# A Trainium2 encoder block: sums of weights and lower parts of keys change engine, and two products change places

## The chip, the cores and the metric

One core of a Trainium2 chip runs the kernel. The metric is the device time of one execution in microseconds (us). Three executions of the kernel before took 1936.4, 1937.48 and 1934.06 us; the median is 1936.4. TensorE (PE in the profile) multiplies matrices, VectorE (DVE) and ScalarE (ACT) and GpSimd (POOL) work elementwise, SyncE (SP) issues most of the DMAs.

## The reference

One layer of an encoder: RMS norm, one wide projection, two branches (banded attention, and retention with rotated queries and keys), gates, output projections and a last norm. It is all float32, with 2048 rows and a width of 1024.

```
h = rms_norm(x, norm_gain)
proj = einsum('bsd,df->bsf', h, w_in)          # w_in: 1024 x 7168
q_a, k_a, v_a, g_a, q_r, k_r, v_r, g_r, m_a, m_r = split_columns(proj)
o_a = chunk_band_attention(q_a, k_a, v_a, rel_bias)
branch_a = einsum('bsf,fd->bsd', o_a * silu(g_a), w_out_attn)
qr, kr = rotary(q_r, positions), rotary(k_r, positions)
o_r = retention_chunkwise(qr, kr, v_r, gn_gain)
branch_r = einsum('bsf,fd->bsd', o_r * silu(g_r), w_out_ret)
mixed = sigmoid(m_a) * branch_a + sigmoid(m_r) * branch_r
out = rms_norm(x + einsum('bsd,de->bse', mixed, w_out), final_gain)
```

The change lies in the projection (the einsum with w_in) and in what is done to the rotated keys after it.

## The kernel before

**Exact products from two parts.** Every float32 operand of a matmul is held as an upper part, rounded to the format that PE multiplies fast (names with `wh_`, `h_`; made by a cast on ACT), and a lower part, the rest (`wl_`, `l_`; a subtraction on DVE, for some products on POOL). A product uses three of the four combinations: upper times upper, upper times lower, lower times upper.

**Seven products for eight.** The dense multiplications are done by Strassen's method in Winograd's form (class `Strassen`). For the projection a chunk is 256 columns of w_in, a half of the rows of x is one job, and the quarters of the weight chunk are 4 x 128 rows by 128 columns (128x512 on the chip). Four *sums of weights* are built from the quarters: t1 = b12 - b11, t2 = b22 - t1, t3 = b12 - b22, t4 = b21 - t2 (`SUMS_OF`, made in `sum`, L338). Each product n multiplies one quarter or sum with one of seven operands made from x (`R[m]`, in the traces `r`, an even number for an upper part and the next odd one for its lower part): n = 0 uses b11, 1 uses t2, 2 uses t3, 3 uses b21, 4 uses t1, 5 uses t4, 6 uses b22. A product has twelve matmuls of 128x512: four steps, of which each reads one quarter of R's upper and lower part. It writes a PSUM bank that is named after its place: n = 0 and then 3 write x, 1 writes y, 2 writes v, 4 and then 6 write z, 5 writes w. `gather` takes the banks out: ACT copies x into u2 after n = 0, and DVE adds y, v, z and w into u2, u3 and c22. A bank that is used a second time must have been read first: n = 3 waits for the copy of x, n = 6 for c22 (or, in a job with a different order, for whatever read z).

**Jobs.** w_in's columns are done in four jobs: `p0` (what the two branches need, for the first half of the rows: ten chunks), `g0` (gates of that half, 14 chunks, dense work between attention and retention), then `p1` and `g1` for the second half. In p0 and p1 the chunks 3 and 5 (and in p0 the first two) are of other kinds (`Rows`, `Front`), whose sums of weights are on DVE already. The trace leaves numbers out, so that p0's and p1's chunks are both `p`: a sum is `t_p`, the raw weights `raw_p`.

**Order.** The dense products of all jobs stand in one list, `seq`; `dense` runs through it. Ahead of each product it emits the loads and the sums and parts of a product some places later (`prime`, `prepare`, three ahead). Each load is due at a fixed number of places ahead of the chunk's first product (`begins[...]`); p1's first chunk has its own places, at - 9 and at - 6 (L640). What is deferred by `later` comes out after a number of steps, a step being a quarter of a product. All engines run their instructions in program order, and each queue waits at its head.

**Where p1 begins.** At the end of g0 chunk 13 (`g_13`) the operands R, too, are filled anew, from the second half of the rows: a DMA brings them (`r <- cs`), ACT casts the upper parts, and DVE subtracts in place for the lower parts (`r_81 <- r_81,r_80` and so on, four pieces for each of seven). p1's first two chunks are done together, product by product.

**Rotated keys.** In p0 and p1 the keys of the retention branch are rotated (`ep_rotated`) in place, on DVE. Then `parted` makes their parts: ACT copies the upper part (`h_k`), and `low` subtracts the lower part (`l_k`) on the engine that it is given, DVE for queries and POOL for keys, and issues the DMAs that store both. `turn` transposes the keys on PE into a bank of its own, which ACT and DVE empty into `kdt_k`. The rotated parts of keys feed the state of the retention in `krs` and `kds`.

Of the kernel before, what the change touches and what calls it, by code (L numbers as in the profile page):

```python
# [16 lines left out]
ALU = mybir.AluOpType  # L17
# [56 lines left out]
def hybrid_kernel(  # L74
# [30 lines left out]
    def r32(ap):  # L105
        return ap.bitcast(F32)
# [7 lines left out]
    def E(name, dt=F32, shape=(P, 512)):  # L114
        return epool[0].tile(list(shape), dt, tag="e", name=name)

    def TR(name):
        return xpool[0].tile([P, 512], F32, tag="tr", name=name)

    def D(name, shape, dt=F32):  # L120
        return dram.tile(list(shape), dt, name=name)
# [31 lines left out]
    pe, act, dve, pool = Ordered(nc.tensor), Sometimes(nc.scalar), Sometimes(nc.vector), Sometimes(nc.gpsimd)  # L153
# [23 lines left out]
    krscr = [[D(f"krs_{c}_{b}", [2, 2, 4, 32, 2, T], F32R) for b in range(NB)] for c in range(2)]  # L177
    qrscr = [[D(f"qrs_{c}_{b}", [2, 4, 32, 2, 2, T], F32R) for b in range(NB)] for c in range(2)]
# [66 lines left out]
    def later(n, fn):  # L245

        order[0] += 1
        deferred.append((steps[0] + n, order[0], fn, free[0]))
        deferred.sort(key=lambda e: e[:2])
# [8 lines left out]
    def put(lag, dst, src):  # L258

        later(lag, lambda: dma(dst, src))  # L260
# [75 lines left out]
    class Strassen(Chunk):  # L336
# [5 lines left out]
        def sum(self, dst, one, two, ring=None):  # L342
            b = self.b
            if dst in b:
                return
            name = f"{dst}_{self.job.name}_{self.c}"
            t = wp.tile([P, 4, P], F32, tag="t", bufs=SUMS, name=name) if ring is None else \
                ring(name).rearrange("p (k c) -> p k c", k=4)
            b[dst] = self.shaped(t)
            pool.tensor_tensor(b[dst], b[one], b[two], ALU.subtract)  # L350

        def before(self):

# [257 lines left out]
    seq = []  # L611

    def prime(n):

        while ready[0] < min(n, len(seq)):
            _, ch, k = seq[ready[0]]
            ch.prepare(k)
            ready[0] += 1
            if ahead[0] and strict[0] and ready[0] + 1 < len(seq):
                _, ch, k = seq[ready[0] + 1]  # L620
                if isinstance(ch, Strassen):
                    ch.sums(k)

    def dense(jobs):
        chunks = [ch for job in jobs for ch in job.chunks]
        following = dict(zip(chunks, chunks[1:]))
        starts = [k for k, (job, ch, n) in enumerate(seq) if isinstance(ch, Plain) and ch.at(n)[2] == 0]
        count, begins = {}, {}
        for at, (job, ch, n) in enumerate(seq):
            if isinstance(ch, Strassen):  # L630
                begins.setdefault(ch, at)
        sooner = {at - lead: (ch, [j]) for ch, at in begins.items()
                  for j, lead in enumerate(ROW_LEADS if isinstance(ch, Rows) else RAW_LEADS)}
        one, two_, three = jobs[2].chunks[:3]
        for ch in (one, two_, three):
            for lead in RAW_LEADS:
                sooner.pop(begins[ch] - lead)
        two_.raw, three.raw = [], []
        at = begins[one]
        sooner[at - 9], sooner[at - 6] = (one, [0]), (one, [1])  # L640

        first_out = jobs[-1].chunks[0]
        at = begins[first_out]
        for lead in RAW_LEADS:
            sooner.pop(at - lead)
        sooner[at - 8], sooner[at - 5] = (first_out, [0]), (first_out, [1])
        operands = {begins[ch] - 2: ch for ch in begins if ch.job.before}
        for at, (job, ch, n) in enumerate(seq):
            free[0] = job.name[0] == "g"
            count[ch] = count.get(ch, 0) + 1  # L650
            if at in sooner:
                ch2, js = sooner[at]
                if ch2.raw is None or js[0]:
                    len(ch2.raw or ()) == js[0] and ch2.load(js)
            if count[ch] == job.when + 1 and ch in following and following[ch].raw is None and not isinstance(ch, Rows):
                following[ch].load()
            prime(at + ahead[0] + 1)
            while starts and starts[0] <= at + job.lead:
                _, ch2, n2 = seq[starts.pop(0)]
                ch2.before(n2)  # L660
            if at in operands:
                operands[at].before()
            for _ in ch.product(n):
                yield True
                free[0] = job.name[0] == "g"
            for fn in hooks.get((job.name, ch.c, n), ()):
                fn()
            yield True
# [326 lines left out]
    def halves(t):  # L995
        return r32(t).rearrange("p (u n) -> p u n", u=2)

    def two(name, shape=(P, 512)):
        return [E(f"{n}_{name}", F32R, shape) for n in "hl"]
# [100 lines left out]

        return epilogue

    def parted(xs, nm, at, eng, dst):

        ws = {}

        def high(n):
            ws[n] = two(f"{nm}_{n}")
            act.copy(ws[n][0], xs[n])

        def low(n):
            eng.tensor_tensor(ws[n][1], xs[n], r32(ws[n][0]), ALU.subtract)
            for i in range(2):
                put(PUT, dst(i, n), halves(ws[n][i]))

        for n in range(2):
            later(at + n, lambda n=n: high(n))
            later(at + 4 + 2 * n, lambda n=n: low(n))

    def queries(cc, b, xs, nm, late):  # L1120
        parted(xs, nm, late + 9, dve, lambda i, h: r32(qrscr[cc][b][:, :, :, h, i]).rearrange("u i c t -> (i c) u t"))

    def keys(cc, b, xs, nm, late):
        parted(xs, nm, late + 9, pool, lambda i, h: r32(krscr[cc][b][:, i, :, :, h]).rearrange("u i c t -> (i c) u t"))

        def turn(u):
            pk = TR(f"trkr_{nm}_{u}")
            v = pk.rearrange("p (t i c h) -> p t h i c", t=2, i=4, h=2)
            for t in range(2):
                for h in range(2):  # L1130
                    pe.transpose(v[:, t, h], xs[h][:, (2 * u + t) * P:(2 * u + t + 1) * P], ident)
            pk = pk.rearrange("p (t i d) -> p i t d", t=2, i=4)
            kt = []

            def high(n):
                kt.append(E(f"kdt_{nm}_{u}_{n}", F32R, (P, 2, 2, P)))
                act.copy(kt[n][:, :, :, 0:HD], pk[:, 2 * n:2 * n + 2])

            def low(n):
                dve.tensor_tensor(  # L1140
                    kt[n][:, :, :, HD:P], pk[:, 2 * n:2 * n + 2], r32(kt[n][:, :, :, 0:HD]), ALU.subtract
                )
                put(PUT, r32(kdscr[2 * cc + n][b][:, u]), r32(kt[n]).rearrange("p i t c -> p i (t c)"))

            for n in range(2):
                later(2 + n, lambda n=n: high(n))
                later(5 + n, lambda n=n: low(n))

        for u in range(2):
            later(late + 18 + 4 * u, lambda u=u: turn(u))  # L1150
# [719 lines left out]
    end, at = {}, 0  # L1870
# [4 lines left out]
    def hook(name, c, n, fn):  # L1875
        hooks.setdefault((name, c, n), []).append(fn)
# [14 lines left out]
    for n, m in ((4, 4), (5, 5), (6, 2), (7, 6)):  # L1891
        hook("br1", 3, n, lambda n=n, m=m: place_wo(m, *((1, 1) if n < 6 else (n - 4, 2))))

    stream = [dense(jobs)]
    seq.extend((job, ch, n) for job in jobs for ch, n in job.seq)
    for j in (jobs[0], jobs[2]):
        for i in range(2):
            hook(j.name, i, 1 if j is jobs[2] else (0, 1, 1), lambda j=j, i=i: j.chunks[2].load([i]))
# [50 lines left out]
    for key in ("b11", "b12", "b21", "b22"):  # L1949
        ch.b[key] = E(f"{key}_p1", shape=(P, 4, P))  # L1950
        j, h = int(key[1]) - 1, int(key[2]) - 1
# [83 lines left out]
```

## Time and profile before

| | before |
|---|---|
| median of three executions | 1936.4 us |
| the profiled execution | 1934.51 us |
| its span | 1932.7 us |
| DVE, ACT, POOL busy | 70%, 48%, 46% |
| instructions in the span | 31908 |

Times of instructions are given from the span's start. In the page and in the views below, a tile's name without numbers stands for a group; `DVE l_k` is an instruction that writes l_k. In a row of the timeline the brackets give how long the engine was idle ahead of it and what released it: `[1.52 <-DVE c_g L143]`. All instructions carry L143, the line of the helper that records them, so one goes by tiles. `x2` joins two instructions, and the time is that of both. Matmuls overlap; what counts for PE is the distance from one start to the next.

### The profile page before, as it was taken

Reading aid. Unit: us, or ns where it says so; the run is one execution under the profiler, and the core shown is the slowest. Engines: PE = TensorE matmul, PEld = TensorE weight load, DVE = VectorE, ACT = ScalarE, POOL = GpSimd, SP = SyncE. Lnnn points to the kernel's source line nnn. Section 1 sums busy time; section 2 is a strip of 40 time slices with the busy share of each in tenths; the row PEclk is TensorE's granted clock in tenths of the full one; section 3 lists DMA queues with packets and bytes.
Section 4 is the critical chain, followed back from the end, with each engine's and each line's share of the span. In section 5 each row is a group of like instructions: output and inputs, shape, how many; then the busy total and the mean of one; then the engine's idle time right before and its main releaser. Section 6 shows DMA issues by size and latency. Waiting matters only on the chain. (4 is left out here: it accounts for less than half of the span.)

```text
span 1932.7 us, 31908 instructions
## 1 busy us (share of the span) xinstructions
PE 1877.7 (97%) x10437; PEld 1614.5 (84%) x10437; DVE 1353.5 (70%) x2530; ACT 931.1 (48%) x1931; POOL 885.1 (46%) x733
## 2 busy tenths in 40 slices
PE   7999999999999999999999999999999999998998
PEld 6899889888888887899889888888888878886886
DVE  6979788677756558879797777775555654557665
ACT  7555554666655545343333556664555221223554
POOL 0313515546546664223515444544564115547775
PEclk9999999999999999999999999999999999999999
DMA  6586876565659988675666555555998999976673
GB/s 196 165 269 204 264 262 223 182 192 171 173 158 282 272 243 286 197 252 186 206 236 216 161 162 175 161 157 161 290 269 270 323 345 328 325 262 222 208 236 132
DMA packets 325557, 435.93 MB, mean 226 GB/s; under 512 B 29880, under 2 KB 191184, under 8 KB 325392
## 3 DMA queue, kind: packets, MB, share of 16 engines
q1 hardware_dynamic: 260096, 368.35, 59.6%
q10 hardware_dynamic: 65296, 65.55, 11.1%
q8 instruction: 83, 1.36, 0.3%
q14 instruction: 82, 0.67, 0.1%
HBM read 288.14 MB, written 145.64 MB: 224 GB/s over the span
## 5 line engine op out<-in xcount | busy, mean ns | idle before, releaser
L143 POOL TENSOR_SCALAR pr<-pr,rsum 128x640 f32<-128x640 f32 (+4 forms) x128 | 96.1, 751 | 213.7 <-DVE ptl L143 104.8
L143 PE MATMUL ps_g_z<-r,wh_g 128*128 128x512 f32 x448 | 143.7, 402 | 2.7 <-DVE c_g L143 2.7
L143 PE MATMUL ps_g_x<-r,wh_g 128*128 128x512 f32 x448 | 143.2, 401 | 1.2 <-ACT u_g L143 1.1
L143 DVE CUSTOM_DVE_ANT_0 pr<-wide,bt 128x640 f32<-128x640 f32 (+4 forms) x128 | 94.3, 736 | 62.4 <-PE wide L143 55.6
L143 ACT ACTIVATE pr<-pr,mn 128x640 f32<-128x640 f32 (+4 forms) x128 | 98.0, 766 | 81.4 <-DVE mn L143 81.4
L143 DVE TENSOR_TENSOR ptl<-tp,pth 128x384 fp32r<-128x384 f32 x168 | 96.1, 573 | 41.3 <-ACT pth L143 37.4
L143 ACT CAST pth<-tp 128x384 fp32r<-128x384 f32 x168 | 84.5, 515 | 68.5 <-PE tp L143 65.6
L143 POOL TENSOR_TENSOR l_vr<-vrt,h_vr 128x512 fp32r<-128x512 f32 x32 | 47.2, 1476 | 117.0 <-ACT h_vr L143 69.3
L143 POOL TENSOR_TENSOR sl<-sm,sh 128x384 fp32r<-128x384 f32 x64 | 70.4, 1099 | 58.3 <-ACT sh L143 46.3
L143 PEld LDWEIGHTS tp<-ident,pr 128*128 128x128 f32 x560 | 71.2, 140 | 27.3 <-POOL pr L143 2.8
L143 PE MATMUL po<-pth,va 128*128 128x256 f32 x336 | 92.5, 296 | 1.2 <-DMA va<-vas 0.7
L143 POOL TENSOR_TENSOR wl_g<-t_g,wh_g 128x512 fp32r<-128x512 f32 x56 | 75.0, 1339 | 39.9 <-ACT wh_g L143 33.2
L143 PE MATMUL tp<-ident,pr 128*128 128x128 f32 x560 | 89.1, 272 | 3.0 <-POOL pr L143 1.9
L143 ACT CAST wh_p<-raw_p 128x512 fp32r<-128x512 f32 x111 | 68.0, 619 | 49.9 <-PE ps_p_y L143 15.5
L143 DVE TENSOR_TENSOR wl_p<-raw_p,wh_p 128x512 fp32r<-128x512 f32 x111 | 86.2, 783 | 7.4 <-ACT wh_p L143 6.9
L143 DVE TENSOR_TENSOR sm<-sr,dm 128x384 f32<-128x384 f32 x64 | 35.6, 556 | 78.5 <-DMA dm<-in_dmask_dram 28.2
L143 PE MATMUL wide<-ka,qa 128*128 128x384 f32 (+1 forms) x448 | 88.3, 313 | 2.2 <-DVE mn L143 2.1
L143 PEld LDWEIGHTS wide<-ka,qa 128*128 128x128 f32 x448 | 74.6, 188 | 18.6 <-DVE mn L143 8.7
L143 PE MATMUL po<-ptl,va 128*128 128x256 f32 x336 | 88.3, 284 | 1.4 <-DVE ptl L143 0.2
L143 PE MATMUL ps_g_x<-r,wl_g 128*128 128x512 f32 x224 | 88.2, 394 | 0.0
L143 PE MATMUL ps_g_z<-r,wl_g 128*128 128x512 f32 x224 | 88.1, 393 | 0.0
L143 PEld LDWEIGHTS ps_g_x<-r,wh_g 128*128 128x128 f32 x448 | 75.8, 189 | 10.7 <-ACT u_g L143 2.5
(930 smaller groups left out, 6217.3 us busy)
## 6 DMA issues: line engine op xcount, KB each, us to landing
raw_g<-in_w_in_dram ACTq DMA_DIRECT2D x56, 512.0 KB, 5.1
raw_p<-in_w_in_dram ACTq DMA_DIRECT2D x50, 512.0 KB, 5.7
qa<-qas SPq DMA_DIRECT2D x128, 128.0 KB, 3.1
qr<-qrs SPq DMA_DIRECT2D x128, 128.0 KB, 4.6
vr<-vrs SPq DMA_DIRECT2D x64, 256.0 KB, 5.4
ka<-kas SPq DMA_DIRECT2D x56, 256.0 KB, 3.2
va<-vas SPq DMA_DIRECT2D x40, 256.0 KB, 3.3
kds<-kdt_k SPq DMA_DIRECT2D x32, 256.0 KB, 3.3
```

The lines of the kernel that those rows point to most:

```text
L143: return tc.keep_in_program_order(op(*a, **k))
```

## The change

It has three parts.

1. In `Strassen.sum`, the sums of weights of the jobs whose name begins with p (`lean`) are subtracted on DVE instead of POOL. There are 56 of them: t1 to t4 of six chunks of p0 (2, 4, 6, 7, 8, 9) and eight of p1 (0, 1, 2, 4, 6, 7, 8, 9). The gates' sums stay on POOL.
2. In `parted`, the lower part is subtracted on DVE always. This moves the 16 `l_k`.
3. In `seq`, where g0 ends and p1 begins, six entries change places: the last product of the gates, g_13's n = 6, goes behind the first of p_0, and the second of p_1 (n = 3) behind p_0's n = 1. p1's first product is thus one place earlier, so `begins[one]` is smaller by one, and the two leads of its raw loads go from 9 and 6 to 8 and 5, which leaves the loads where they were.

```diff
@@ sum @@
-            pool.tensor_tensor(b[dst], b[one], b[two], ALU.subtract)
+            (dve if self.lean() else pool).tensor_tensor(b[dst], b[one], b[two], ALU.subtract)
+
+        def lean(self):
+            return self.job.name[0] == "p"
@@ dense @@
         at = begins[one]
-        sooner[at - 9], sooner[at - 6] = (one, [0]), (one, [1])
+        sooner[at - 8], sooner[at - 5] = (one, [0]), (one, [1])
@@ parted, queries, keys @@
-    def parted(xs, nm, at, eng, dst):
+    def parted(xs, nm, at, dst):
...
-            eng.tensor_tensor(ws[n][1], xs[n], r32(ws[n][0]), ALU.subtract)
+            dve.tensor_tensor(ws[n][1], xs[n], r32(ws[n][0]), ALU.subtract)
...
-        parted(xs, nm, late + 9, dve, lambda i, h: ...)     # queries
+        parted(xs, nm, late + 9, lambda i, h: ...)
...
-        parted(xs, nm, late + 9, pool, lambda i, h: ...)    # keys
+        parted(xs, nm, late + 9, lambda i, h: ...)
@@ where the jobs are put in a row @@
     seq.extend((job, ch, n) for job in jobs for ch, n in job.seq)
+    at = end["g0"] // 4
+    seq[at - 1:at + 5] = [seq[at + k] for k in (0, -1, 1, 2, 4, 3)]
```

On DVE, at the end of p0 where `trkr_k` is emptied (before the transposes of 247 us), the moved instructions stand as follows. `t1_p0_9` to `t4_p0_9` are the sums for chunk 9 and `l_k_1_0_n` the lower parts of the keys.

```order
 L143 TENSOR_TENSOR wl_p0_9_0_3162<-raw_p0_9_0_2970,wh_p0_9_0_3161 128x512
 L143 SCALAR_TENSOR_TENSOR l_qa_0_2_3201<-ps_p0_8_x_3032,h_qa_0_2_3200 128x512
+L143 TENSOR_TENSOR l_k_1_0_0_3181<-xk_1_0_0_2967,h_k_1_0_0_3180 128x512
 L143 TENSOR_TENSOR kdt_k_1_1_1_0_3193<-trkr_k_1_1_1_3167,kdt_k_1_1_1_0_3193 128x4x64
 L143 TENSOR_TENSOR kdt_k_1_1_1_1_3209<-trkr_k_1_1_1_3167,kdt_k_1_1_1_1_3209 128x4x64
 L143 TENSOR_TENSOR u3_p0_8_3147<-ps_p0_8_w_3216,u3_p0_8_3147 128x512
+L143 TENSOR_TENSOR l_k_1_0_1_3190<-u2_p0_7_2846,h_k_1_0_1_3189 128x512
 L143 TENSOR_TENSOR wl_p0_9_4_3214<-t1_p0_9_3082,wh_p0_9_4_3213 128x512
+L143 TENSOR_TENSOR t4_p0_9_3254<-raw_p0_9_1_3000,t2_p0_9_3084 128x512
```

The added rows stand in DVE's one queue now, ahead of evacuations (kdt_k, u3) that used not to stand behind them.

At chunk 4 of p0, at about 115 us, DVE's queue is:

```order
 L143 TENSOR_TENSOR kdt_k_0_0_1_0_1586<-trkr_k_0_0_1_1553,kdt_k_0_0_1_0_1586 128x4x64
 L143 TENSOR_TENSOR wl_p0_3_5_1_1574<-raw_p0_3_10_1092,wh_p0_3_5_1_1573 128x512
+L143 TENSOR_TENSOR t1_p0_4_1619<-raw_p0_4_0_1432 128x512
+L143 TENSOR_TENSOR t2_p0_4_1621<-raw_p0_4_1_1477,t1_p0_4_1619 128x512
 L143 TENSOR_TENSOR kdt_k_0_0_1_1_1595<-trkr_k_0_0_1_1553,kdt_k_0_0_1_1_1595 128x4x64
 L143 TENSOR_TENSOR c22_p0_3_0_1636<-ps_p0_3_z_0_1576,u3_p0_3_0_1539 128x512
```

The sum t2 needs the second half of the raw weights (`raw_p0_4_1`), and a kdt_k and c22 stand behind it.

On PE, where g0 ends and p1 begins, these are the first rows of the products (each stands for twelve), before:

```order
L143 MATMUL ps_g_13_w<-r_84,wh_g_13_5_9404 128x512
...
L143 MATMUL ps_g_13_z<-r_92,wh_g_13_6_9433 128x512
...
L143 MATMUL ps_p_0_x<-r_80,wh_p_0_0_9482 128x512
...
L143 MATMUL ps_p_1_x<-r_80,wh_p_1_0_9537 128x512
...
L143 MATMUL ps_p_0_y<-r_88,wh_p_0_1_9592 128x512
```

and in the change:

```order
L143 MATMUL ps_g_13_w<-r_84,wh_g_13_5_9406 128x512
...
L143 MATMUL ps_p_0_x<-r_80,wh_p_0_0_9433 128x512
...
L143 MATMUL ps_g_13_z<-r_92,wh_g_13_6_9482 128x512
...
L143 MATMUL ps_p_0_x<-r_82,wh_p_0_3_9510 128x512
...
L143 MATMUL ps_p_1_x<-r_80,wh_p_1_0_9537 128x512
...
L143 MATMUL ps_p_0_y<-r_88,wh_p_0_1_9561 128x512
...
L143 MATMUL ps_p_1_x<-r_82,wh_p_1_3_9592 128x512
```

Before, p_0's two products into the bank x (with r_80 and r_82) followed each other, and so did p_1's, and g_13's n = 5 and n = 6. Now another product lies between the two of each pair.

More of the change, by code (lines that the diff above doesn't have):

```diff
@@ L1120, in queries @@
     def queries(cc, b, xs, nm, late):
-        parted(xs, nm, late + 9, dve, lambda i, h: r32(qrscr[cc][b][:, :, :, h, i]).rearrange("u i c t -> (i c) u t"))
+        parted(xs, nm, late + 9, lambda i, h: r32(qrscr[cc][b][:, :, :, h, i]).rearrange("u i c t -> (i c) u t"))
     def keys(cc, b, xs, nm, late):
-        parted(xs, nm, late + 9, pool, lambda i, h: r32(krscr[cc][b][:, i, :, :, h]).rearrange("u i c t -> (i c) u t"))
+        parted(xs, nm, late + 9, lambda i, h: r32(krscr[cc][b][:, i, :, :, h]).rearrange("u i c t -> (i c) u t"))
         def turn(u):
```

## The prediction

> **What bounds the kernel now.** I read the page first, then the list of what TensorE (PE) waited for, then the timeline of each of those places, and last the windows around them.
>
> ```profile
> PE 1877.7 (97%) x10437; PEld 1614.5 (84%) x10437; DVE 1353.5 (70%) x2530; ACT 931.1 (48%) x1931; POOL 885.1 (46%) x733
> ```
>
> PE is busy for 97% of the span, so the change can only win what PE loses. No matmul is removed by it. Which losses belong to the projections is in the list of waits (total us, times, longest):
>
> ```profile
> PE pst L143 <- DVE kdt_k L143: 2.3, 1, 2.3
> PE ps_g_z L143 <- DVE c_g L143: 2.7, 2, 1.5
> PE ps_p_z L143 <- DVE c_p L143: 2.2, 1, 2.2
> PE ps_p_x L143 <- ACT u_p L143: 1.8, 2, 1.2
> PE ps_p_y L143 <- DVE wl_p L143: 0.9, 1, 0.9
> PE ps_p_w L143 <- DVE wl_p L143: 0.9, 1, 0.9
> ```
>
> Most of them end with a VectorE (DVE) instruction, and those that don't lie at the change from the last gate chunk to the second projections ("the junction"). PE's own rows there:
>
> ```profile
> 749.90 0.39 PE L143 MATMUL ps_g_w<-r,wl_g 128*128 128x512 f32 x1
> 751.81 0.70 PE L143 MATMUL ps_g_z<-r,wh_g 128*128 128x512 f32 x2 [1.52 <-DVE c_g L143]
> 758.70 0.73 PE L143 MATMUL ps_p_x<-r,wh_p 128*128 128x512 f32 x2 [1.17 <-ACT u_p L143]
> 765.11 0.73 PE L143 MATMUL ps_p_x<-r,wh_p 128*128 128x512 f32 x2 [0.68 <-ACT u_p L143]
> 785.82 0.50 PE L143 MATMUL ps_p_w<-r,wl_p 128*128 128x512 f32 x1 [0.90 <-DVE wl_p L143]
> ```
>
> Undisturbed, matmuls of 512 columns start 0.227 us apart (from 246.29 to 246.52 in the rows further below), and a product of twelve takes 2.72. From 749.90 to 751.81 are 1.91 us, so the first wait costs 1.91 - 0.23 = 1.68, some 0.16 over its idle time. With that, the four cost 1.52 + 1.17 + 0.68 + 0.90 + 4 x 0.16 = **4.9 us**.
>
> **Why DVE is late.** The windows (PE, PEld, DVE, ACT, POOL busy, granted clock) say that DVE is full there:
>
> ```profile
> 228.00:250.00 22.00, 20.05 (x97) 16.31 (x95) 21.86 (x26) 9.93 (x26) 9.63 (x6) 1.00 0.54 169
> 744.00:790.00 46.00, 41.73 (x180) 33.28 (x179) 45.90 (x61) 24.91 (x46) 18.46 (x11) 1.00 0.65 229
> 952.00:972.00 20.00, 20.00 (x93) 16.55 (x92) 19.45 (x21) 5.29 (x10) 10.83 (x7) 1.00 0.28 96
> ```
>
> What fills it is partly GpSimd (POOL). The timeline of both, where sums of weights run on POOL (DVE first):
>
> ```profile
> 756.40 1.18 DVE L143 TENSOR_TENSOR r<-r,r 128x512 fp32r<-128x512 f32 x1
> 757.51 1.75 DVE L143 TENSOR_TENSOR wl_p<-b_p,wh_p 128x512 fp32r<-128x512 f32 x1
> 759.18 3.48 DVE L143 TENSOR_TENSOR r<-r,r 128x512 fp32r<-128x512 f32 x2
> 762.59 1.78 DVE L143 TENSOR_TENSOR wl_p<-b_p,wh_p 128x512 fp32r<-128x512 f32 x1
> 764.29 2.36 DVE L143 TENSOR_TENSOR r<-r,r 128x512 fp32r<-128x512 f32 x2
> 766.57 0.68 DVE L143 TENSOR_TENSOR wl_p<-t_p,wh_p 128x512 fp32r<-128x512 f32 x1
> 789.90 0.68 DVE L143 TENSOR_TENSOR r<-r,r 128x512 fp32r<-128x512 f32 x1
> 790.50 0.68 DVE L143 TENSOR_TENSOR wl_p<-raw_p,wh_p 128x512 fp32r<-128x512 f32 x1
> ...
> 753.46 3.58 POOL L143 TENSOR_TENSOR t_p<-b_p,b_p 128x512 f32<-128x512 f32 x1 [9.29 <-issue]
> ...
> 763.77 1.72 POOL L143 TENSOR_TENSOR t_p<-b_p,t_p 128x512 f32<-128x512 f32 x1
> ```
>
> Undisturbed, such DVE instructions follow each other every 0.60 us (789.90 to 790.50). Beside POOL's they take 1.7: from 757.51 to 759.18 one, from 762.59 to 764.29 one. Seven instructions take 10.17 us from 756.40 to 766.57 where 7 x 0.60 = 4.2 would do, so the six sums that POOL ran meanwhile (the first and the last are quoted) cost DVE 6.0, about 1.0 to 1.1 each.
>
> **The change, part by part.** *The 56 sums.* What one costs on DVE is seen, since twelve of the same shape run there already:
>
> ```profile
> L143 DVE TENSOR_TENSOR t_p<-raw_p,raw_p x12: 691/692/694, 83.5 to 997.6; 128x512 f32<-128x512 f32 x12
> ...
> L143 POOL TENSOR_TENSOR l_k<-u_p,h_k x8: 1288/1351/1632, 87.7 to 978.0; 128x512 fp32r<-128x512 f32 x8
> ```
>
> So 0.69 long, 0.60 when queued. On a full DVE a moved sum therefore adds 0.60 and takes away about 1.1: **0.5 lighter**. On a DVE with gaps it is hidden. The bounds are a relief of nothing (then +0.60 each) and of 1.29, the length alone (then -0.7); I take 1.1, measured in place. *The 16 lower parts of keys* have the same shape and get the same price; their DMA issues on SP stay in place.
>
> *First projections, 91 and 105 us.* PE waits for a wl_p behind DVE instructions that stood beside an l_k on POOL (ps_p_y <- wl_p in the list, and this one):
>
> ```profile
> 103.65 1.72 DVE L143 TENSOR_TENSOR wl_p<-raw_p,wh_p 128x512 fp32r<-128x512 f32 x1
> 105.43 0.39 PE L143 MATMUL ps_p_v<-wl_p,r 128*128 128x256 f32 x1 [0.35 <-DVE wl_p L143]
> ```
>
> At 105 the late wl_p itself is the slowed one, 1.72 instead of 0.68. With the restart the two cost 0.91 + 0.16 = 1.1 and 0.35 + 0.16 = 0.5, and I let both go: **1.6**. At worst, if an l_k on DVE stands right ahead of each and the slowness was not POOL's, 0.6 is added to each.
>
> *247 us.* Transposes wait until DVE has emptied their bank (kdt_k):
>
> ```profile
> 246.29 0.40 PE L143 MATMUL ps_p_w<-r,wl_p 128*128 128x512 f32 x1
> 246.52 0.62 PE L143 MATMUL ps_p_w<-r,wh_p 128*128 128x512 f32 x2
> ...
> 247.66 0.39 PE L143 MATMUL ps_p_w<-r,wl_p 128*128 128x512 f32 x1
> 250.38 0.99 PE L143 MATMUL pst<-ident,xs 128*128 128x128 f32 x4 [2.34 <-DVE kdt_k L143]
> ...
> 249.71 0.42 DVE L143 TENSOR_TENSOR kdt_k<-trkr_k,kdt_k 128x256 fp32r<-128x256 f32 x1
> ...
> 220.00:260.00 40.00, 37.66 (x176) 31.02 (x175) 35.44 (x46) 20.58 (x48) 19.06 (x12) 0.96 0.69 217
> ```
>
> The wait costs 250.38 - 247.66 - 0.23 = 2.5. Behind it the granted clock falls: 0.96 over 40 us is 1.6 us of PE lost. All six of POOL's instructions in the window from 228 to 250 (x6) move: four sums and two l_k. DVE gets 6 x 0.5 = 3.0 lighter, kdt_k ends at 250.13 - 3.0 = 247.1, and PE arrives at 247.9: 0.8 to spare. Wait and clock loss go: **4.1**; what is late next is that same kdt_k, if the relief is under 0.4 each.
>
> *972 us.* The same picture with c_p, of POOL's seven instructions from 952 to 972 six move (the seventh, of yr, stays):
>
> ```profile
> 974.57 0.70 PE L143 MATMUL ps_p_z<-r,wh_p 128*128 128x512 f32 x2 [2.17 <-DVE c_p L143]
> ```
>
> The cost is 2.17 + 0.16 = **2.3**; c_p comes 3.0 earlier, with 0.7 to spare.
>
> *The junction.* The new order puts a product (2.72) between the two that had to follow each other through one bank. This covers c_g (1.7), and the copies u_p (1.3 and 0.8). What stays is DVE's amount of work: the last lower part of r (789.90, ended at 790.58) feeds p_0's n = 6. The gates' w ends its starts with 749.90, so the next product starts at 750.13; p_0's n = 6 is the fourteenth from there, without waits at 750.13 + 13 x 2.72 = 785.5, and needs that piece with its eleventh matmul, 10 x 0.227 = 2.3 later, at 787.8. DVE is lighter by 6.0 - 6 x 0.60 = 2.4, so it is there at 788.2: about 0.5 of wait remains, **4.4** of 4.9 go. If DVE gets no lighter, 2.8 remain and the gain is 2.1. One new chain arises: the gate's t4 stands one product later, and its weight reaches POOL later:
>
> ```profile
> 740.63 1.84 POOL L143 TENSOR_TENSOR wl_g<-t_g,wh_g 128x512 fp32r<-128x512 f32 x1 [1.88 <-ACT wh_g L143]
> ```
>
> It ended at 742.47; 2.72 later is 745.2, and PE needs it with the third matmul of the gates' w, at 750.13 - 2.72 + 0.45 = 747.9, so I cost it at nothing with 2.6 us of cover.
>
> *The sum*: 1.6 + 4.1 + 2.3 + 4.4 = 12.4. Against the profiled execution (1934.51, of which the span is 1932.7) this gives 1922.1. The median of the runs, 1936.4, lies 1.9 above that execution, and I carry this over: **1924.0**.
>
> **The rivals.** *Half the relief* (chance 0.20): a moved instruction frees 0.85, not 1.1, since POOL sums beside idle DVE moments cost it less. Then 247 leaves 1.0 of wait without the clock loss (3.1 gained), 972 gains 1.5, the junction 3.3 (DVE ends 1.6 late), the first two 1.6: 9.5, so 1926.9. For it speaks that half of the l_k on POOL last 1.35 or less (the median of their row), so they met a DVE that left room; against it the six sums at the junction, measured together.
>
> *Nothing moves* (0.09): other work, such as ScalarE's copies, bounds the same places and PE waits as long under other names: 1935 or so. Against it, ACT is busy for 24.91 of 46 us at the junction.
>
> *DVE was full and POOL free* (0.05): if POOL's rows are long only because DVE's are, each moved instruction is 0.60 more on a full engine. Then 247 and 972 get 3.6 longer each, and at the junction DVE ends at 790.58 + 3.6 = 794.2, 6.4 late against 4.9 lost now; less 1.6, this is +7.1, 1943.5. Against it, DVE rows of 1.7 beside POOL's, and 0.68 alone. The Trainium skill ("Perfetto Trace Analysis", section "Optimizing Scalar/DVE Operations") speaks for this side: a saturated DVE is to be relieved by giving work to ScalarE or even GpSimd, the opposite of this change, though it adds that between DVE and GpSimd it might not help, because of a shared port. By its first half the time would be this rival's 1943.5, by its second the forecast; the rows agree with the second.
>
> *A blocked queue* (0.08), also slower: DVE works in order, and a sum that waits for its half of the raw weights holds up all behind it, evacuations and kdt_k above all. POOL waited for just this:
>
> ```profile
> DMA raw_p<-in_w_in_dram: 16.0, 5
> 114.77 1.50 POOL L143 TENSOR_TENSOR t_p<-raw_p,t_p 128x512 f32<-128x512 f32 x1 [5.01 <-DMA raw_p<-in_w_in_dram]
> 115.03 0.42 DVE L143 TENSOR_TENSOR kdt_k<-trkr_k,kdt_k 128x256 fp32r<-128x256 f32 x1
> ```
>
> If the loads land as late against DVE's places, five waits of 16.0 / 5 = 3.2 on average reach PE less 0.8 of cover each: 12.0, and 1.6 of clock each: 20.0, less 12.4, so 1944. It decides from 12.4 us of such waits on. Against it: DVE comes to its place later than POOL did. At the worst place the half landed at 114.77 and DVE gets there at about 115.6, behind kdt_k (115.03, 0.42): 0.8 to spare.
>
> **How the numbers follow.** The forecast has 0.58, with its own range of 1920 (another clock loss missing, no wait at the junction) to 1926. A measurement of this kernel tells some 0.2%, 3.9 us, from no change, so "faster" is below 1932.5. Forecast and half the relief make faster 0.78; the same 0.09; the two slower rivals 0.13. The range takes in the forecast, half the relief and part of no change: 1920 to 1934.
>
> **What would show it.** In the changed profile DVE rows beside former POOL sums should be 0.68, not 1.7; the waits pst<-kdt_k, ps_p_z<-c_p, ps_g_z<-c_g (at the junction) and ps_p_x<-u_p should be gone, and the clock 1.00 from 220 to 260. At the junction a wait of up to 1 us near 787 should remain. I am wrong if PE waits for wl_p or c_p behind a t_p on DVE that itself waits for raw_p, or if DVE is still full with PE waits of 2 us at 247 or 972.

## The result, and the profile after

The changed kernel took 1922.31 us (median of five runs, 1918.53 to 1926.96); the kernel before took 1935.7 (five runs). The ratio is 0.9928, with a 95% interval from 0.9911 to 0.9945: faster by 13.4 us. The forecast was 1924.0, in a range from 1920 to 1934.

The profiled execution took 1926.96 us, the slowest of the five. In its list of what TensorE (PE) waited for (total us, times, longest), the named waits of before are gone (pst <- kdt_k, p_z <- c_p, p_x <- u_p, p_y and p_w <- wl_p) or, for c_g, down to one of 0.7, and others stand there:

```profile
PE pst L143 <- ACT xs L143: 2.7, 1, 2.7
PE sr L143 <- DMA qr<-qrs: 2.6, 2, 2.1
...
PE ps_p_z L143 <- DVE u_p L143: 0.7, 1, 0.7
...
PE ps_g_z L143 <- DVE c_g L143: 0.7, 1, 0.7
...
PE ps_p_z L143 <- DVE r L143: 0.5, 1, 0.5
```

The c_g that is left belongs to another gate chunk, at 695 us. Here are the windows of the changed kernel (us; PE, PEld, DVE, ACT and POOL busy; granted clock):

```profile
228.00:250.00 22.00, 22.00 (x108) 18.27 (x107) 20.08 (x34) 12.95 (x33) 0.00 (x0) 1.00 0.64 207
744.00:790.00 46.00, 46.00 (x204) 38.09 (x203) 45.51 (x72) 28.36 (x53) 3.55 (x3) 1.00 0.75 263
952.00:972.00 20.00, 20.00 (x94) 16.55 (x93) 19.79 (x33) 7.08 (x15) 1.62 (x1) 1.00 0.25 88
220.00:260.00 40.00, 40.00 (x193) 33.07 (x192) 35.47 (x58) 22.37 (x51) 4.44 (x3) 1.00 0.75 239
```

From 744 to 790 PE is busy throughout, where it missed 4.3 us before. VectorE (DVE) is as full as ever (45.51 of 46), but it got 72 instructions through instead of 61. From 228 to 250 GpSimd (POOL) is silent, DVE does 34 instead of 26, and from 220 to 260 the clock is 1.00 instead of 0.96. The timeline of DVE and PE in the same execution shows the moved sums and the places of the forecast:

```profile
758.40 0.69 DVE L143 TENSOR_TENSOR t_p<-b_p,b_p 128x512 f32<-128x512 f32 x1
759.13 0.69 DVE L143 TENSOR_TENSOR t_p<-b_p,t_p 128x512 f32<-128x512 f32 x1
759.74 0.68 DVE L143 TENSOR_TENSOR r<-r,r 128x512 fp32r<-128x512 f32 x1
...
246.68 0.42 DVE L143 TENSOR_TENSOR kdt_k<-trkr_k,kdt_k 128x256 fp32r<-128x256 f32 x1
...
247.59 0.60 PE L143 MATMUL pst<-ident,xs 128*128 128x128 f32 x4
...
278.57 1.35 PE L143 MATMUL pst<-ident,xs 128*128 128x128 f32 x4 [2.73 <-ACT xs L143]
...
791.39 0.50 PE L143 MATMUL ps_p_z<-r,wh_p 128*128 128x512 f32 x1 [0.50 <-DVE r L143]
```

A sum on DVE costs 0.60 to 0.73 from start to start, and its neighbours are no longer 1.7 long. kdt_k ends at 247.10, where 247.1 was forecast, and the transposes (pst) start at 247.59 without a wait. But 31 us later another group of transposes waits 2.73 us, for xs.

### The profile page after: what moved, and what is told of

The parts are those of the page before. It is cut to its first block, busy times and chain, and to the rows that moved or that the text cites. A ratio compares the mean times of both kernels' runs of the same rounds, so it can differ in the third digit from the quotient of the medians.

```text
span 1925.2 us, 31831 instructions
## 1 busy us (share of the span) xinstructions
PE 1879.2 (98%) x10437; PEld 1617.7 (84%) x10437; DVE 1355.6 (70%) x2602; ACT 930.3 (48%) x1931; POOL 771.7 (40%) x661
## 5 line engine op out<-in xcount | busy, mean ns | idle before, releaser
L143 POOL TENSOR_TENSOR yr<-yr,rb 128x512 f32<-128x512 f32 x8 | 11.7, 1467 | 191.1 <-DVE yr L143 100.1
L143 POOL TENSOR_TENSOR t_g<-raw_g,t_g 128x512 f32<-128x512 f32 x56 | 73.8, 1318 | 28.7 <-DVE wl_g L143 10.6
```

Of the source, the lines that this page charges most:

```text
L143: return tc.keep_in_program_order(op(*a, **k))
```

## The experiments

All are compared with the kernel before on the same chip, in several rounds. The kernel before took 1931 to 1935 us in them, by the medians; the ratios count.

**The parts alone.** Each of three kernels keeps one part of the change and undoes the others; a fourth undoes only the order. The first keeps the sums:

```diff
-            dve.tensor_tensor(ws[n][1], xs[n], r32(ws[n][0]), ALU.subtract)
+            (pool if nm[0] == "k" else dve).tensor_tensor(ws[n][1], xs[n], r32(ws[n][0]), ALU.subtract)
...
-        sooner[at - 8], sooner[at - 5] = (one, [0]), (one, [1])
+        sooner[at - 9], sooner[at - 6] = (one, [0]), (one, [1])
...
-    at = end["g0"] // 4
-    seq[at - 1:at + 5] = [seq[at + k] for k in (0, -1, 1, 2, 4, 3)]
```

> Only the 56 sums of weights go to VectorE; keys' lower parts stay on GpSimd, and the order at the start of p1 is the old one. Theory (GpSimd's instructions slow a full VectorE by about 1.1 us each, the work itself costs it 0.6): the waits at 91 and 105 us stay (1.6); four of six moved instructions are gone at 247 and 972, so VectorE is 2.0 lighter there and the waits shrink from 2.5 and 2.3 to 0.5 and 0.3, without the clock loss; at the junction the waits for c_g and u_p stay mostly (3 us of 4.9). Gain about 7.5 us, ratio 0.996. Rival (VectorE full, GpSimd's work free): the waits at 247 and 972 grow by 2.4 each, ratio 1.002 or more. Rival (the order alone makes the gain): ratio 1.000, waits as before.

Measured: ratio 0.9975 (0.9961 to 0.9989). Its waits before 300 us:

```profile
PE pst L143 <- ACT xs L143: 2.0, 1, 2.0
PE ps_p_y L143 <- DVE wl_p L143: 0.9, 1, 0.9
PE pst L143 <- DVE kdt_k L143: 0.6, 1, 0.6
PE ps_p_z L143 <- ACT wh_p L143: 0.6, 1, 0.6
PE ps_p_v L143 <- DVE wl_p L143: 0.4, 1, 0.4
```

kdt_k leaves 0.6 where 0.5 was expected, and the two wl_p stay. At the junction the waits for u_p (1.9) and c_g (0.7) stay too, near the 3 expected. The gain, 4.8 us, is smaller than the 7.5. Of what is missing, 2.0 us of wait for xs can be seen, which has appeared, and the clock of 0.98 from 220 to 300 that came with it.

The second keeps only the keys' lower parts:

```diff
-            (dve if self.lean() else pool).tensor_tensor(b[dst], b[one], b[two], ALU.subtract)
+            pool.tensor_tensor(b[dst], b[one], b[two], ALU.subtract)
...
-        sooner[at - 8], sooner[at - 5] = (one, [0]), (one, [1])
+        sooner[at - 9], sooner[at - 6] = (one, [0]), (one, [1])
...
-    at = end["g0"] // 4
-    seq[at - 1:at + 5] = [seq[at + k] for k in (0, -1, 1, 2, 4, 3)]
```

> Only the 16 lower parts of keys go to VectorE; the sums stay on GpSimd, old order. Theory: the waits at 91 and 105 us go (1.6); two of six moved instructions at 247 and 972 make VectorE 1.0 lighter, so 1.5 and 1.3 of wait remain, and the clock loss at 250 goes (1.6) if 1.5 us is too short for it; the junction stays as before. Gain about 4 to 5 us, ratio 0.9975. Rival (VectorE full, GpSimd's work free): waits at 91, 105, 247 and 972 grow by 0.6 to 1.2 each, ratio 1.002.

Measured: 0.9974 (0.9963 to 0.9985), 5.0 us. The waits at 91 and 105 are gone, as the theory says, and 1.2 of the wait for kdt_k is left:

```profile
PE pst L143 <- ACT xs L143: 1.9, 2, 1.7
PE pst L143 <- DVE kdt_k L143: 1.2, 1, 1.2
```

Sixteen instructions win as much as the 56 sums do, by the ratios. That this is so because they stand where DVE is late is likely, but no run tries it. The junction was expected as before; in this execution, the slowest of its twelve, PE waited 3.5 us for u_p there instead of 1.8.

The third keeps only the order; the sums and the keys' lower parts are on POOL again:

```diff
-            (dve if self.lean() else pool).tensor_tensor(b[dst], b[one], b[two], ALU.subtract)
+            pool.tensor_tensor(b[dst], b[one], b[two], ALU.subtract)
...
-            dve.tensor_tensor(ws[n][1], xs[n], r32(ws[n][0]), ALU.subtract)
+            (pool if nm[0] == "k" else dve).tensor_tensor(ws[n][1], xs[n], r32(ws[n][0]), ALU.subtract)
```

> Only the six products at the start of p1 change places, and the two loads' leads with them; sums and keys' lower parts stay on GpSimd. Theory: the waits for c_g and u_p at the junction (3.85) go, but VectorE, no lighter, leaves a wait of about 2.8 for the last lower part of r (p_z <- r); gain 2.1 us; 91, 105, 247 and 972 as before. Ratio 0.999. Rival (the order alone makes the gain): ratio 0.993, and no wait for r.

Measured: 0.9994 (0.9983 to 1.0005): no change that can be told. The waits for u_p are gone, but from 740 to 800 PE waits for DVE at four other places:

```profile
PE ps_p_y L143 <- DVE wl_p L143: 1.0, 1, 1.0
PE ps_p_w L143 <- DVE wl_p L143: 0.7, 1, 0.7
PE ps_p_x L143 <- DVE wl_p L143: 0.5, 1, 0.5
PE ps_p_x L143 <- DVE r L143: 0.5, 1, 0.5
```

Together these make 2.7, about the 2.8 of the theory, though spread over four waits instead of one at the end.

The fourth undoes only the order and the leads:

```diff
-        sooner[at - 8], sooner[at - 5] = (one, [0]), (one, [1])
+        sooner[at - 9], sooner[at - 6] = (one, [0]), (one, [1])
...
-    at = end["g0"] // 4
-    seq[at - 1:at + 5] = [seq[at + k] for k in (0, -1, 1, 2, 4, 3)]
```

> Sums and keys' lower parts on VectorE as in the change, but the old order at the start of p1. Theory: 91, 105, 247 and 972 as in the change (8.0 us gained), at the junction the waits of c_g and u_p stay for the most part, 2 to 3 us. Gain 9 to 10 us, ratio 0.995. Rival (order does nothing for itself, a lighter VectorE removes c_g and u_p too): ratio as the change, 0.993, and no wait for c_g or u_p. Rival (order makes the gain): 1.000.

Measured: 0.996 (0.9945 to 0.9974), 7.7 us; u_p leaves 1.8 us (1.2 and 0.6) and c_g, with the one at 695, 1.3. So by the ratios the order is worth 1.2 us (which can't be told from nothing) on a DVE that is as heavy as before, and 4 to 6 on a lighter one: 0.996 against the 0.9928 and 0.9937 of the whole. The intervals are too wide to show that the parts help each other. The traces say it more finely: every one of them has the same 10437 matmuls, and so the start of the n-th matmul can be compared. From 740 to 800 us of the time before, the order alone gains 1.1 us, the rest without the order 2.1, and both together 4.7 and 4.9 in two profiles. So together they gain about 1.6 more than one by one, as far as single executions show it.

**The whole once more, and the sums at the junction.** The sixth kernel leaves the eight sums of p1's first two chunks on POOL:

```diff
-            return self.job.name[0] == "p"
+            return self.job.name[0] == "p" and not (self.job.name == "p1" and self.c < 2)
```

> The change once more, as it is. Theory: the wait of the transposes for xs at about 279 us (pst <- ACT xs, 2.7 in its first profile, 1.7 to 2.0 in three of the parts) is systematic: a load of x that the wait for kdt_k at 247 us used to hide. It should be there again, 1.5 to 3 us. The wait for qr at 704 us (2.1) is chance and may be missing. Ratio 0.993. Rival (the wait for xs is chance): under 0.5 here.

Measured: 0.9937 (0.992 to 0.9954), median 1921.77. The wait for xs is there again, 2.6 us, so it is no chance; the one for qr is not.

> The change, but the eight sums of p1's first two chunks stay on GpSimd. Theory: VectorE gets 2.4 us heavier at the junction (six sums at 1.1 less 0.6 each, plus what t1 and t2 of the first chunk cost), so the wait for r in the product n = 6 of p_0 (0.5 us idle in the change) grows to about 2.5 to 3, and little else changes: 2 to 3 us slower than the change, ratio 0.9945. Rival (the sums' engine doesn't matter here): as the change, wait 0.5.

Measured: 0.9954 (0.9936 to 0.9971), median 1924.33, 2.6 us slower than the whole beside it (the intervals overlap, so the time alone doesn't show it). The wait was one of 2.02, but not for r:

```profile
759.02 0.50 PE L143 MATMUL ps_p_y<-r,wl_p 128*128 128x512 f32 x1 [2.02 <-DVE wl_p L143]
...
756.70 1.72 POOL L143 TENSOR_TENSOR t_p<-b_p,t_p 128x512 f32<-128x512 f32 x1
...
757.22 1.75 DVE L143 TENSOR_TENSOR wl_p<-t_p,wh_p 128x512 fp32r<-128x512 f32 x1
```

POOL's sum (756.70) and the wl_p that PE waited for (757.22, 1.75 long) lie beside each other. The size is as expected, the place earlier.

**Is it GpSimd being quiet?** In the seventh kernel DVE's program is the change's, instruction by instruction, and POOL does the sums too, into a tile that nobody reads (a useless sum is called a twin):

```diff
+            if self.lean():
+                h = b[dst].shape[-1] // 2
+                w = h * 7 // 8
+                twin = wp.tile([P, 4, 56], F32, tag="twin", bufs=1, name=f"twin_{name}")
+                to = twin.rearrange("p k (i c) -> p k i c", i=4) if self.job.paired[self.c] else twin
+                for n in range(2):
+                    pool.tensor_tensor(to, b[one][..., n * h:n * h + w], b[two][..., n * h:n * h + w], ALU.subtract)
```

> The change, and GpSimd computes each of the 56 sums too, for nothing, into a tile that nobody reads (in two halves, 7/8 of the columns). VectorE's program is the same, instruction by instruction. Theory (contention): each twin slows a full VectorE by about 1 us: kdt_k at 247 comes 4 late with 0.8 to spare, so 3 us of wait and perhaps the clock loss come back, c_p at 972 the same, and at the junction 6 us: 10 to 14 us slower than the change, ratio 0.999 to 1.002. Rival (the gain comes from when the sums are done, not from GpSimd being quiet): as the change, 0.993.

Measured: 1.0098 (1.0082 to 1.0113), 30 us slower than the change beside it, over twice what any theory gave. To see whether POOL's reading did it, the ninth kernel replaced the twin's subtraction:

```diff
-                    pool.tensor_tensor(to, b[one][..., n * h:n * h + w], b[two][..., n * h:n * h + w], ALU.subtract)
+                    pool.memset(to, 0.0)
```

> As the doubled sums, but GpSimd fills its useless tile with zeros, twice for each sum, and reads nothing. They wait for no weights, so they run earlier than the twins did. Theory (it is GpSimd's reading that holds VectorE up): VectorE's instructions beside a memset keep their 0.68 us, and the time is the change's, ratio 0.993. Rival (any access of GpSimd to the memory holds VectorE up, writing too): rows of 1 us or more beside memsets, and ratio 0.996 to 1.005.

Measured: 1.0009 (0.9998 to 1.002), 14 us or so above the change: the rival's time, but not its rows, for the memsets slow nothing on DVE. These are POOL and DVE in that execution:

```profile
740.17 4.76 POOL L143 MEMSET twin_t_p<- 128x224 f32 x14
...
740.71 0.67 DVE L143 TENSOR_TENSOR t_p<-raw_p,t_p 128x512 f32<-128x512 f32 x1
741.31 0.67 DVE L143 TENSOR_TENSOR rt<-rt,rt 32x512 f32<-32x512 f32 x1
```

and PE loses time at the end of the kernel too, where no such instruction runs. The windows of three executions from 1600 to 1720 us count the matmuls. The whole change:

```profile
1600.00:1720.00 120.00, 120.00 (x531) 99.34 (x531) 63.70 (x82) 25.17 (x43) 65.31 (x45) 1.00 0.86 296
```

With memsets:

```profile
1600.00:1720.00 120.00, 120.00 (x518) 97.33 (x517) 65.71 (x82) 26.02 (x44) 63.60 (x45) 1.00 0.90 306
```

531 matmuls against 518 in 120 us, 0.226 us each against 0.232, at the same clock and without a wait. What the two kernels share is the useless tile of 896 bytes per partition, which pushes the tiles behind it, those of wh and wl, by as much. Two kernels tell this apart. The tenth has the tile alone:

```diff
+            if name == "t1_p0_2":
+                twin = wp.tile([P, 4, 56], F32, tag="twin", bufs=1, name="twin")
+                pool.memset(twin, 0.0)
```

> The change, with a tile of 896 bytes per partition added among the weights' tiles and filled once; no other instruction. In both kernels with such a tile the parts of the weights (wh, wl) lay 896 bytes further, and PE's matmuls of 512 columns started 0.232 us apart instead of 0.227 all through the projections. Theory (that place of the weights' parts slows PE): 0.232 here too, ratio 0.999 to 1.001. Rival (GpSimd's useless instructions did it): 0.227 and ratio 0.993.

Measured: 1.0001 (0.9987 to 1.0016), and in its profile

```profile
1600.00:1720.00 120.00, 120.00 (x518) 97.26 (x517) 63.92 (x80) 25.95 (x44) 62.73 (x45) 1.00 0.88 300
```

So the tile alone costs 12 to 14 us, all that the memsets had seemed to. The eleventh kernel repeats the doubled sums with the tile in another pool, behind the weights:

```diff
-                twin = wp.tile([P, 4, 56], F32, tag="twin", bufs=1, name=f"twin_{name}")
+                twin = small.tile([P, 4, 56], F32, tag="twin", bufs=1, name=f"twin_{name}")
```

> The doubled sums again, with GpSimd's useless tile behind all weights, so that these stay where the change has them. Theory (contention, measured without the slower matmuls): matmuls 0.227 us apart, VectorE's rows beside a twin 1.1 instead of 0.6 apart, waits of some 3 us at 247 and 972 and 5 at the junction; all in all 12 to 18 us slower than the change, ratio 1.000 to 1.003. Rival (the doubled sums were slow only through the place of the weights): as the change, 0.993.

Measured: 1.0037 (1.0026 to 1.0048), 0.010 above the change's 0.9937 and 0.9928, that is 19 to 21 us. Now nothing differs from the change but POOL's twins (and the place of tiles behind the weights). The waits for kdt_k and c_p are back at their places, and at the junction PE waits for DVE again:

```profile
PE pst L143 <- DVE kdt_k L143: 3.7, 1, 3.7
...
PE ps_p_z L143 <- DVE wl_p L143: 2.8, 2, 1.5
PE ps_p_z L143 <- DVE c_p L143: 1.8, 1, 1.8
PE ps_p_z L143 <- DVE r L143: 1.6, 2, 0.8
PE ps_p_y L143 <- DVE wl_p L143: 1.2, 2, 0.9
```

and DVE's instructions beside the twins (POOL 762.93 to 767.26 here) last 1.15 instead of 0.68:

```profile
763.44 1.15 DVE L143 TENSOR_TENSOR wl_p<-t_p,wh_p 128x512 fp32r<-128x512 f32 x1
764.52 1.15 DVE L143 TENSOR_TENSOR t_p<-raw_p,raw_p 128x512 f32<-128x512 f32 x1
...
762.93 2.20 POOL L143 TENSOR_TENSOR twin_t_p<-raw_p,raw_p 128x224 f32<-128x224 f32 x2
765.20 2.06 POOL L143 TENSOR_TENSOR twin_t_p<-b_p,b_p 128x224 f32<-128x224 f32 x2
```

The theory gave 12 to 18. By the starts of the same matmuls, this kernel falls behind the second profile of the change by 3.3 us up to 105, where the theory had nothing, by 1.9 more up to 290, by 9.7 from 740 to 800, where it had some 5, and by 2.7 at 972. ScalarE waited for a twin twice: for 5.8 us at 209, which cost the matmuls next to nothing (0.2 from 110 to 230), and for 2.4 at 231, which may have a part in what is lost at 247. The rival, that POOL's quiet does not matter, is out. Added to the 12 to 14 for the place of the tile, the 19 to 21 make a little more than the 30 of the seventh kernel.

**The wait that took the place of kdt_k.** The loads of x's last piece are issued by SyncE. In the first profile after, its queue and ScalarE's rows were:

```profile
273.67 2.16 SPq L143 DMA_DIRECT2D xs<-in_x_dram  x3
...
276.95 0.38 SPq L143 DMA_DIRECT2D xs<-in_x_dram  x1
...
278.11 1.86 ACT L143 ACTIVATE xs<-xs,rs 128x128 f32<-128x128 f32 x6 [8.11 <-DMA xs<-in_x_dram]
```

ScalarE had waited 8.11 us for the first load, and PE waited for ScalarE. The eighth kernel issues them from ScalarE's queue:

```diff
-                dma(a, rows.rearrange("(t p) c -> p t c", p=P))
+                (act.dma_start if k == 3 else dma)(a, rows.rearrange("(t p) c -> p t c", p=P))
```

> The change, but the four loads of x's last piece (xs, k = 3) are issued from ScalarE's queue, not SyncE's, which is late there. Theory (SyncE's queue issues the load too late): it lands 5 us or more earlier, the wait of pst for xs at 279 us goes (2 to 3 us, and the clock loss with it): 3 us faster than the change, ratio 0.991 to 0.992. Rival (the DMA engines are full there, so it lands as late): the wait stays, ratio 0.993. Rival (ScalarE is held up by the issue, waiting for a free tile): PE waits for wh_p or u_p instead, ratio 0.994 or more.

Measured: 0.992 (0.9906 to 0.9934), median 1917.87 beside 1921.77 of the whole change: the fastest of all, though the intervals overlap a little. Its first issue:

```profile
266.91 0.38 ACTq L143 DMA_DIRECT2D xs<-in_x_dram  x1
```

The wait is gone, and the clock is whole again. In the windows from 220 to 300, first the whole change, as run beside it:

```profile
220.00:300.00 80.00, 77.41 (x442) 67.80 (x441) 68.67 (x109) 40.61 (x91) 9.10 (x6) 0.98 0.77 255
```

and then the loads by ScalarE:

```profile
220.00:300.00 80.00, 80.00 (x482) 71.02 (x481) 71.58 (x113) 43.01 (x95) 10.95 (x8) 1.00 0.80 267
```

2.6 us of PE and 1.6 us of clock (0.02 of 80) are back; by the medians 3.9.

## Why the prediction was right, and where it wasn't

- **That POOL slows a full DVE, and a moved instruction makes it lighter.** Right, and shown: with DVE's program unchanged, POOL's twins alone bring 19 to 21 us. The rival of a full DVE and a free POOL is out: DVE did more instructions in the same time. That nothing moves is out too, since the waits are gone. With half the relief, kdt_k would have ended 1.5 us earlier than before, at 248.6; it ended at 247.10, of which 0.3 was a lead that this execution had at 230 already.
- **The waits at 91 and 105** (1.6): gone, and it is the keys' part that removes them (with the keys alone they are gone, with the sums alone they stay). At 105 the same matmuls lead by only 0.2 us in the first profile after and 0.7 in the second. A wait near 78 that nobody forecast came with the sums, 0.7 in the first profile and 0.4 in the second. Its cause was not tried.
- **247 us** (4.1): the mechanism was right, and so was the time of kdt_k, to 0.3 us. The net gain was not: the transposes at 279 wait for xs, 2.7 and 2.6 us in two profiles, and the clock falls there instead (0.98 over 220 to 300). This gives back all of it, and is the term that was mis-sized. By the same matmuls, the second profile leads that of before by 4.9 us at 255 and by 0.6 at 283, and it led by 0.8 at 230, so nothing of the 4.1 is kept. The prediction said that kdt_k itself would be next if the relief were small; next was a load of x, which before had landed just in time behind the wait for kdt_k. The run with the loads by ScalarE shows that it was the issue on SyncE's queue that came too late.
- **972 us** (2.3): gone, and with the sums or the keys alone too (nothing left, and 0.2), where the prediction's price per instruction left 0.3 and 1.3.
- **The junction** (4.4 of 4.9): right in all three parts. c_g and u_p are covered by the order, and a wait for r remains, 0.5 and 0.3 against the forecast 0.5; the order alone gives little (1.1 by the starts of matmuls, against 2.1), for without a lighter DVE the wait for it comes back elsewhere.
- **The chain of the gates' t4** was free, as costed; PE had no wait for wl_g there.
- **A blocked queue**: in the changed profile a sum on DVE waited for raw weights once, 1.06 us at 268, and PE had no wait from 108 to 240. The rival is out. Its price was too high from the start: the 16.0 us in five waits, taken from the view of the tile t_p, hold waits of ScalarE (5.4 us at 806) and DVE (0.4) as well. POOL itself had waited three times, 10.2 us (at 108, 115 and 214), and with these the rival would have come out at about no change instead of 1944.
- **The sum**: 12.4 forecast; 13.4 and 12.2 measured (by medians, and by the ratio in the second comparison). But it is not the forecast's sum, and that the two agree so well is in part luck. In the second profile (1919.92, against 1934.51) the starts of the same matmuls lead by 4.9 us at 255, 0.6 at 283, 4.4 at 717, 9.6 at 786, 11.5 at 974 and 14.3 at 1785 of the time before. So the first projections kept 0.6, the junction brought 5.2 (forecast 4.4) and 972 with what lies between 1.9 (forecast 2.3); 3.8 came between 283 and 717 and 2.8 after 974, where the change moves nothing. The kernel with the order alone does the same as the kernel before in these stretches, and its profile gained 3.3 us from 283 to 717 and 3.4 from 985 to 1785; the first profile of the change lost 2.7 in the first stretch. So these gains are differences between single executions, and no run shows them to be the change's. The places that the prediction named bring about 7 and 8 us in the two profiles. The ratios say 12 to 14, and their intervals begin at 9 and 11; what brings the rest was not found. The forecast was near because what was given back at 279 and what came elsewhere nearly cancelled.

## What to carry to other kernels

Where VectorE is full, look at what GpSimd does beside it before counting GpSimd's time as free: an elementwise instruction with two operands there can cost VectorE more than doing it on VectorE. After removing a wait, follow the next load on a slow queue, for a wait that was hidden behind the first takes its place; here a load issued 7 us earlier from another queue won it back. An order and a relief can need each other: the order alone gave nothing that could be told, the relief alone 7.7 us, both 12 to 13, though the intervals leave room for a plain sum. And a total that comes out as forecast doesn't show that its terms did: compare the starts of the same instructions, place by place, in more than one profile.

## What was not expected of the hardware

The place of a tile decided the speed of the matmuls. With the parts of the weights 896 bytes further, matmuls of 512 columns started 0.232 us apart instead of 0.226 (518 against 531 in 120 us), with the same clock and no waits, and the kernel lost 12 to 14 us, as much as the whole change had won. In the eleventh kernel, with the same tile behind the parts, they are 531 again. Which places are good or bad, and why, was not tried.

GpSimd's writing alone did not slow VectorE: beside 14 memsets in a row (740.17 to 744.93) VectorE's instructions kept their 0.67 us. Nor did its reading slow those that take an operand from PSUM: in the eleventh kernel, from 60 to 300 and from 740 to 1010 us, all 45 TENSOR_TENSORs of 128x512 with such an operand that ran beside GpSimd took at most 0.69 us, while 70 of 123 with both operands in SBUF took over 1 us there, and none of the 314 that ran while GpSimd was idle took over 0.70. The Trainium skill ("SBUF — State Buffer", section "SBUF: two separate sides") says that a VectorE instruction with two operands in SBUF contends with a GpSimd instruction that reads SBUF; the rows agree: 1.15 beside the reading twins, 0.67 beside the memsets.
